# A hybrid decoder step on one core: the input's load order and the cost figures of the host scheduler

## The chip, the core and the metric

The kernel runs on one core of a Trainium2 chip. The metric is the device time of one execution in microseconds (us). Three runs of the kernel before gave 2321.42 to 2325.67 us, with a median of 2323.08 us.

## What is computed

One inference step of a decoder of two layers in float32, for one new sequence of 512 tokens (the prompt) and for eight running sequences with four new tokens each (the sample, 32 rows), which share all weights. Layer A runs sparse attention (compressed, selected and window branches) beside gated linear attention; layer C is a gated recurrence. Cut to what matters here:

```python
def layer_a(x, ...):
    h = rmsnorm(x, norm_w)
    q, kv, g_br, z_a, q_b, k_b, v_b, lr_b, z_b = split_cols(h @ w_in, A_SIZES)
    ...
    full = jnp.concatenate([past_kv, new_rows], axis=1)      # sample: 512 cached rows, in pages
    o_a = nsa_attend(q, gates, full, win_kv, ...) * jax.nn.silu(z_a)
    ...
    y = x + jnp.concatenate([o_a, o_b], axis=-1) @ w_out
def layer_c(x, ...):
    q, f, i, z = split_cols(rmsnorm(x, norm_w) @ w_in, C_SIZES)
    ...
    return x + o @ w_out, s
```

The model width is 2048, a cached page holds 128 rows, and `past_kv` is gathered through a page table whose entries are known only when the kernel runs.

## The kernel before

All 544 rows (512 prompt, 32 sample) go through each weight together. Activations lie transposed, in 16 k-tiles of 128 channels by 544 rows. Each operand of a product is split into a rounded part and a remainder (`xh`, `xl` for the activations, `wh`, `wl` for the weights), and each k-tile takes three products, in two column halves of 272: six TensorE (PE) instructions, named gm below. Weights come in tiles `wr` of 512 KB through SyncE's (SP) DMA queue, with three buffers; ScalarE (ACT) casts `wh`, VectorE (DVE) subtracts `wl`.

**The order.** A host-side list scheduler, the class `Kern`, emits the program. It keeps a modelled time for PE (`clk`), for the other engines (`et`) and for the tiles (`rdy`, `last`). `account` charges each instruction a modelled cost; a transfer gets an issue cost and a time on one shared `et["dma"]`. Side tasks (input, attention, recurrences) are generators that emit their next instruction when the model says that its operands are there, and the long runs of gm are emitted in between. So the figures of the model set the order of the instructions on each engine and nothing else: on the chip each engine works through its list in that order and waits on semaphores.

**The input.** `load_x` loads one quarter (512 channels) of the input as five tiles `xt`: four of the prompt (256 KB each) and one of the sample. `load0` and `load1`, at the first weight tiles of the first two blocks, call it. `input_task` transposes the quarters on PE, copies them out (`res`), scales them by the norm weight (`xh`, `xl`), and squares them on ACT for the norm; the norm's factor is spread over partitions by products `dg,ones`. Before the first transposes PE runs 24 products of a tile of ones (`onesr`). Small parameters (`cvr`) come over GpSimd's (POOL) queue.

**The decode attention.** `decode` attends from the sample to the cache at the end of layer A's projections, beside the last blocks of gm. It works through four items: two groups of sequences with paged rows (tile `pg`), then the same two with window rows (tile `pw`). An item transposes eight K tiles (`s<-ident,pg`), multiplies by the queries (`kct,qd`), takes the softmax, transposes the weights (`pd`) and multiplies eight V tiles in two halves (`pg,ptd`). At most `PAGES` = 9 tiles are in flight. `cache_tile` loads a `pg` tile as two DMAs of 128 KB on SP, each behind a read of its page number from the page table (`value_load`); the two paged items take 64 such DMAs. After it comes the output projection of layer A, whose operands (`oh`, `ol`) `parts_a` writes.

All engine calls pass through one helper, so their lines read L84; products are L211, transposes L215. The program after the change has 20 lines more above `input_task`'s callers, and there the two read L214 and L218.

Of the kernel before, what the change touches and what calls it, by code (L numbers as in the profile page):

```python
# [16 lines left out]
AF = mybir.ActivationFunctionType  # L17
# [3 lines left out]
P = 128  # L21
D = 2048
KT = D // P
TP = 512
# [39 lines left out]


LAT = 200.0
SQGAP = 900.0
COST = {"V": (62.0, 1.05), "A": (100.0, 0.84), "G": (110.0, 2.2), "S": (50.0, 0.0)}
FAST = {"tensor_scalar", "tensor_scalar_max", "memset"}

# [24 lines left out]
class Kern:  # L95
    def __init__(self, ctx, tc, a, o):
        self.ctx, self.tc = ctx, tc
        self.nc = Chip(self, tc.nc)
        self.a, self.o = a, o
        self.clk = 0.0  # L100
        self.et = {"V": 0.0, "A": 0.0, "G": 0.0, "S": 0.0, "dma": 0.0}
        self.rdy, self.last = {}, {}
        self.ring, self.held = {"s": [], "gm": []}, {}
        self.lanes, self.order = {}, []
        self.flags = set()
        self.uid = 0
        self.R = None
# [36 lines left out]
    def account(self, eng, op, args, kw):  # L144
        aps = [x for x in list(args) + list(kw.values()) if hasattr(x, "tensor") and hasattr(x, "shape")]
        if not aps or op in ("value_load", "preload_act_table_set"):
            return
        outs = [x for x in (kw.get("out", args[0] if args else None), kw.get("accum_out")) if x is not None]
        names = {x.name for x in outs}
        start = max([self.et[eng]] + [self.rdy.get(x.name, 0.0) + LAT for x in aps if x.name not in names]  # L150
                    + [max(self.rdy.get(x, 0.0), self.last.get(x, 0.0)) + LAT for x in names])
        n = 1
        for x in aps:
            k = 1
            for d in x.shape[1:]:
                k *= d
            n = max(n, k)
        if op == "dma_start":
            self.et[eng] = start + (1040.0 if eng == "G" else 60.0)
            self.et["dma"] = max(self.et["dma"], start) + n * outs[0].shape[0] * 4 / 300.0  # L160
            end = self.et["dma"] + 1900.0
        else:
            fix, per = COST[eng]
            if eng == "V" and op in FAST:
                per = 0.55
            if op == "reciprocal":
                per = 6.8
            end = self.et[eng] = start + fix + per * n
        for x in aps:
            self.last[x.name] = max(self.last.get(x.name, 0.0), end)  # L170
            if x.name in self.held and x.name not in names:
                self.held[x.name] -= 1
                if not self.held[x.name]:
                    del self.held[x.name]
        for x in names:
            self.rdy[x] = end

    def pe(self, cost, out, ins):
        start = max([self.clk] + [self.rdy.get(x.name, 0.0) + LAT for x in ins])
# [427 lines left out]
    def load_x(self, c):  # L607

        nc, a = self.nc, self.a
        for i in range(5):  # L610
            t = (self.r if c < 3 else self.g)("xt", [P, 512])
            s = slice(c * 512, (c + 1) * 512)
            if i < 4:
                nc.sync.dma_start(t, a["x_prompt"][0, i * P:(i + 1) * P, s])
            else:
                nc.sync.dma_start(t[:TS], a["x_sample"].rearrange("b t d -> (b t) d")[:, s])
            self.xt[(c, i)] = t

    def input_task(self):
# [6 lines left out]
        def squares(c, xt):  # L626
            junk = self.g("junk", [P, 512])
            for i in range(5):
                n = P if i < 4 else TS
                nc.scalar.activation(junk[:n], xt[i][:n], AF.Square, accum_out=ss[:n, i, c:c + 1])  # L630
                yield self.later(SQGAP)
            self.sqn += 1

        for c in range(4):
            xt = [self.xt.pop((c, i)) for i in range(5)]
            yield self.at(*xt)
            psb = self.bank(reads=4)
            for q in range(4):
                self.tr(psb[:, q * TS:(q + 1) * TS], xt[4][:TS, q * P:(q + 1) * P], self.ident[:TS, :TS])
            for q in range(4):  # L640
                kt = 4 * c + q
                yield self.at(banks=1)
                psa = self.bank()
                for i in range(4):
                    self.tr(psa[:, i * P:(i + 1) * P], xt[i][:, q * P:(q + 1) * P], self.ident)
                w = self.w_a[:, kt:kt + 1]
                hi, lo = self.g("xh", dt=F32R), self.g("xl", dt=F32R)
                res = self.g("res")
                self.cp(res[:, :TP], psa)
                self.cp(res[:, TP:T], psb[:, q * TS:(q + 1) * TS])  # L650
                self.scale(hi, res, w)
                nc.vector.scalar_tensor_tensor(lo, res, w, hi.bitcast(F32), op0=ALU.mult, op1=ALU.subtract)
                self.xhl[kt] = (hi, lo)
                self.store(self.xres[kt], res)
# [1105 lines left out]
    def layer_a(self):  # L1760
# [163 lines left out]
        def load0(i, t):  # L1924
            self.load_x(0 if i == 0 else 2)
            x0(i, t)
            if i == 0:
                self.small_loads()

        def load1(i, t):  # L1930
            x1(i, t)
            self.load_x(1 if i == 0 else 3)
        blocks[0].load, blocks[1].load = load0, load1
        blocks[0].now = True
        return blocks
# [85 lines left out]
    def program(self):  # L2021
# [25 lines left out]
        def parts_a():  # L2047
            gens = []
            for n, kt in enumerate(order_a):
                fl = [] if n < 4 else ["xfree"]  # L2050
                if kt >= 8:
                    gens.append(self.parts(kt, self.spill[kt], self.g, *fl))
                else:
                    gens.append(self.parts(kt, None, lambda s, dt=F32: self.r(s, dt=dt), "rmid"))
# [111 lines left out]
```

## Time and profile before

| what | us |
|---|---|
| median of three runs | 2323.08 |
| the profiled execution, its own time | 2324.13 |
| span of that execution's trace | 2322.4 |
| PE busy | 2288.0 |
| ACT busy | 1012.1 |
| DVE busy | 1394.5 |

The profiled execution is 1.05 us above the median and 1.7 us above its own span. The trace is read by engine: the timeline gives each stretch of like instructions with its start, its length and, in brackets, the idle time before it and what ended it. PE's instructions overlap, so the time of one is read from the starts of its neighbours.

### The profile page before, as it was taken

Reading aid. Unit: us, or ns where it says so; the run is one execution under the profiler, and the core shown is the slowest. Engines: PE = TensorE matmul, PEld = TensorE weight load, DVE = VectorE, ACT = ScalarE, POOL = GpSimd, SP = SyncE. Lnnn points to the kernel's source line nnn. Section 1 sums busy time; section 2 is a strip of 40 time slices with the busy share of each in tenths; the row PEclk is TensorE's granted clock in tenths of the full one; section 3 lists DMA queues with packets and bytes.
Section 4 is the critical chain, followed back from the end, with each engine's and each line's share of the span. In section 5 each row is a group of like instructions: output and inputs, shape, how many; then the busy total and the mean of one; then the engine's idle time right before and its main releaser. Section 6 shows DMA issues by size and latency. Waiting matters only on the chain.

```text
span 2322.4 us, 50208 instructions
## 1 busy us (share of the span) xinstructions
PE 2288.0 (99%) x20744; PEld 2231.0 (96%) x20744; DVE 1394.5 (60%) x2998; ACT 1012.1 (44%) x2105; POOL 33.5 (1%) x92
## 2 busy tenths in 40 slices
PE   8999999999999999999999999999999999999997
PEld 8999999999999999889999999999999999999997
DVE  5454577774664663454435777777777777775333
ACT  6343344443443443443333455444455444455333
POOL 4000000000000000000000000000000000000000
PEclk9999999999999999999999999999999999999999
DMA  7654434434113135754464333333333333333333
GB/s 238 165 158 143 125 95 110 116 102 131 46 51 88 47 108 158 217 156 134 138 197 142 102 88 108 93 93 101 97 98 93 93 94 102 93 98 120 107 101 115
DMA packets 429685, 270.69 MB, mean 117 GB/s; under 512 B 12326, under 2 KB 415632, under 8 KB 429328
## 3 DMA queue, kind: packets, MB, share of 16 engines
q1 hardware_dynamic: 428144, 256.65, 38.3%
q0 software_dynamic: 704, 8.72, 1.1%
q8 instruction: 163, 2.67, 0.5%
q10 hardware_dynamic: 608, 2.11, 0.2%
q14 instruction: 66, 0.54, 0.1%
HBM read 234.34 MB, written 41.42 MB: 119 GB/s over the span
## 4 chain that ended last, share of the span: by engine, by line
PE 93%; DMA 2%; ACT 1%; POOL 1%; DVE 1%; issue 1%; SPq 1%; DVEq 0%; POOLq 0%; ACTq 0%
PE gm L211 79%; PE s L211 11%; PE s L215 4%; DMA wr<-in_c_w_in_dram 1%; DMA pg<-in_cache_kv_dram 1%; SPq L84 1%; ACT junk L84 0%; DVE ol L84 0%; POOL mkt L84 0%; ACT wh L84 0%; POOL cvr L84 0%; ACT oh L84 0%; ACT e L84 0%; ACT res L84 0%; POOL lmb L84 0%
## 5 line engine op out<-in xcount | busy, mean ns | idle before, releaser
L211 PE MATMUL gm<-xh,wh 128*128 128x272 f32 x3744 | 802.5, 296 | 6.8 <-ACT wh L84 6.8
L211 PE MATMUL gm<-xh,wl 128*128 128x272 f32 x3744 | 775.8, 289 | 0.0
L211 PE MATMUL gm<-xl,wh 128*128 128x272 f32 x3744 | 775.5, 288 | 0.2
L84 DVE TENSOR_TENSOR wl<-wr,wh 128x512 fp32r<-128x512 f32 x660 | 450.5, 686 | 461.1 <-ACT wh L84 460.3
L211 PEld LDWEIGHTS gm<-xh,wh 128*128 128x128 f32 x3744 | 588.9, 189 | 19.4 <-ACT wh L84 7.8
L84 ACT CAST wh<-wr 128x512 fp32r<-128x512 f32 x660 | 401.3, 616 | 468.3 <-PE gm L211 436.0
L211 PEld LDWEIGHTS gm<-xl,wh 128*128 128x128 f32 x3744 | 588.2, 188 | 0.6 <-DVE xl L84 0.6
L211 PEld LDWEIGHTS gm<-xh,wl 128*128 128x128 f32 x3744 | 587.1, 188 | 0.8 <-DVE wl L84 0.6
L211 PE MATMUL gm<-oh,wh 128*128 128x272 f32 (+2 forms) x1024 | 218.3, 292 | 4.1 <-ACT oh L84 3.6
L211 PE MATMUL gm<-ol,wh 128*128 128x272 f32 (+2 forms) x1024 | 214.9, 289 | 0.5 <-DVE ol L84 0.5
L211 PE MATMUL gm<-oh,wl 128*128 128x272 f32 (+2 forms) x1024 | 215.2, 289 | 0.0
L211 PEld LDWEIGHTS gm<-oh,wh 128*128 128x128 f32 x1024 | 162.1, 189 | 5.5 <-ACT oh L84 4.0
L211 PEld LDWEIGHTS gm<-ol,wh 128*128 128x128 f32 x1024 | 162.3, 189 | 0.9 <-DVE ol L84 0.9
L211 PEld LDWEIGHTS gm<-oh,wl 128*128 128x128 f32 x1024 | 161.9, 189 | 0.0
L211 PE MATMUL gm<-ch,wh 128*128 128x258 f32 (+1 forms) x256 | 76.1, 297 | 0.0
L211 PE MATMUL gm<-ch,wl 128*128 128x258 f32 (+1 forms) x256 | 76.0, 297 | 0.0
L211 PE MATMUL gm<-cl,wh 128*128 128x258 f32 (+1 forms) x256 | 76.0, 297 | 0.0
L84 ACT ACTIVATE lv<-lv 128x512 f32<-128x512 f32 (+1 forms) x100 | 61.5, 634 | 29.6 <-DVE lv L84 28.5
L84 ACT COPY o<-s 128x32 f32<-128x32 f32 (+1 forms) x48 | 18.6, 387 | 127.7 <-PE s L211 127.7
L84 ACT ACTIVATE e<-e 128x544 f32<-128x544 f32 x96 | 63.1, 657 | 16.1 <-DVE e L84 14.0
L84 DVE TENSOR_TENSOR lv<-b 128x256 f32<-128x256 f32 (+2 forms) x160 | 68.9, 488 | 0.7
L84 DVE TENSOR_TENSOR rt<-gm,rt 128x544 f32<-128x544 f32 (+2 forms) x33 | 23.3, 707 | 63.7 <-PE gm L211 61.8
(382 smaller groups left out, 2552.4 us busy)
## 6 DMA issues: line engine op xcount, KB each, us to landing
wr<-in_c_w_in_dram SPq DMA_DIRECT2D x128, 512.0 KB
wr<-in_a_w_in_dram SPq DMA_DIRECT2D x104, 512.0 KB
pg<-in_cache_kv_dram SPq DMA_DIRECT2D x128, 128.0 KB
wr<-in_a_cmp_w_dram SPq DMA_DIRECT2D x32, 512.0 KB
wr<-in_a_w_out_dram SPq DMA_DIRECT2D x32, 512.0 KB
wr<-in_c_w_out_dram SPq DMA_DIRECT2D x32, 512.0 KB
out_dram<-s SPq DMA_DIRECT2D x48, 256.0 KB
pw<-in_cache_win_dram SPq DMA_DIRECT2D x32, 256.0 KB
```

The costliest lines, as they stand in the source:

```text
L84: return f(*args, **kw)
L211: return self.nc.tensor.matmul(out, lhsT, rhs, start=start, stop=stop, **kw)
L215: return self.nc.tensor.transpose(out, in_, ident, **kw)
```

## The change

The model: a DMA issue on SP or ACT costs 440 ns instead of 60; a DMA into a tile that is already being loaded no longer waits in the model for the one before it; POOL's DMAs no longer occupy the shared transfer time. The input: each quarter's sample tile is loaded first, two of the first quarter's prompt tiles are issued by ACT, and the last quarter is loaded right behind the third; squares are emitted only where the model's ACT is less than 300 ns ahead of PE; the first k-tile is scaled by ACT straight out of PSUM and 12 more `onesr` products follow its transposes. `parts_a` lets three parts instead of four go without waiting for `xfree`.

```diff
-SQGAP = 900.0
+SQGAP = 300.0
...
-        self.rdy, self.last = {}, {}
+        self.rdy, self.last, self.loading = {}, {}, set()
...
         start = max([self.et[eng]] + [self.rdy.get(x.name, 0.0) + LAT for x in aps if x.name not in names]
-                    + [max(self.rdy.get(x, 0.0), self.last.get(x, 0.0)) + LAT for x in names])
+                    + [max(self.rdy.get(x, 0.0), self.last.get(x, 0.0)) + LAT for x in names if x not in self.loading])
...
         if op == "dma_start":
-            self.et[eng] = start + (1040.0 if eng == "G" else 60.0)
-            self.et["dma"] = max(self.et["dma"], start) + n * outs[0].shape[0] * 4 / 300.0
-            end = self.et["dma"] + 1900.0
+            self.et[eng] = start + (1040.0 if eng == "G" else 440.0)
+            t = max(self.et["dma"], start) + n * outs[0].shape[0] * 4 / 300.0
+            if eng != "G":
+                self.et["dma"] = t
+            end = t + 1900.0
...
             self.rdy[x] = end
+            (self.loading.add if op == "dma_start" else self.loading.discard)(x)
...
-        for i in range(5):
+        for i in (4, 0, 1, 2, 3):
...
-                nc.sync.dma_start(t, a["x_prompt"][0, i * P:(i + 1) * P, s])
+                q = nc.scalar if c == 0 and i > 1 else nc.sync
+                q.dma_start(t, a["x_prompt"][0, i * P:(i + 1) * P, s])
...
                 n = P if i < 4 else TS
+                while self.et["A"] > self.clk + SQGAP:
+                    yield self.later(300.0)
                 nc.scalar.activation(junk[:n], xt[i][:n], AF.Square, accum_out=ss[:n, i, c:c + 1])
-                yield self.later(SQGAP)
+                yield self.later(300.0)
...
-            psb = self.bank(reads=4)
+            psb = self.bank(reads=4 if c else 5)
+            warm = self.bank() if c == 0 else None
...
-                psa = self.bank()
+                psa = self.bank(reads=2 if kt == 0 else 1)
...
-                self.cp(res[:, :TP], psa)
-                self.cp(res[:, TP:T], psb[:, q * TS:(q + 1) * TS])
-                self.scale(hi, res, w)
+                if kt == 0:
+
+                    nc.scalar.activation(hi[:, :TP], psa, AF.Copy, scale=w)
+                    nc.scalar.activation(hi[:, TP:T], psb[:, :TS], AF.Copy, scale=w)
+                    nc.vector.tensor_copy(res[:, :TP], psa)
+                    nc.vector.tensor_copy(res[:, TP:T], psb[:, :TS])
+                    for k in range(12):
+                        self.mm(warm[:, :P], self.onesr, self.onesr)
+                    nc.vector.tensor_copy(self.sm("warm", [P, 1], bufs=1), warm[:, 0:1])
+                else:
+                    self.cp(res[:, :TP], psa)
+                    self.cp(res[:, TP:T], psb[:, q * TS:(q + 1) * TS])
+                    self.scale(hi, res, w)
...
             if i == 0:
                 self.small_loads()
+            else:
+                self.load_x(3)
...
-            self.load_x(1 if i == 0 else 3)
+            if i == 0:
+                self.load_x(1)
...
-                fl = [] if n < 4 else ["xfree"]
+                fl = [] if n < 3 else ["xfree"]
```

**PE in the decode attention, between the two halves of the first item's V tiles.** Before, the first half (its last four products) is followed by gm:

```order
L211 MATMUL s_12105<-pg_11420,ptd_12048 32x256
L211 MATMUL s_12105<-pg_11766,ptd_12048 32x256
L211 MATMUL s_12105<-pg_11787,ptd_12048 32x256
L211 MATMUL s_12105<-pg_11821,ptd_12048 32x256
L211 MATMUL gm_12011<-xh_513,wh_12007 128x272 x2
L211 MATMUL gm_12011<-xl_514,wh_12007 128x272 x2
L211 MATMUL gm_12011<-xh_513,wl_12008 128x272 x2
```

and now by the second half's products:

```order
L214 MATMUL s_12045<-pg_11436,ptd_12035 32x256
L214 MATMUL s_12045<-pg_11752,ptd_12035 32x256
L214 MATMUL s_12045<-pg_11773,ptd_12035 32x256
L214 MATMUL s_12045<-pg_11807,ptd_12035 32x256
L214 MATMUL s_12045<-pg_11828,ptd_12035 32x256
L214 MATMUL s_12045<-pg_11863,ptd_12035 32x256
L214 MATMUL s_12045<-pg_11884,ptd_12035 32x256
L214 MATMUL s_12045<-pg_11923,ptd_12035 32x256
```

The 108 gm that stood between the halves have gone behind them. Over the whole stretch, from the first `s<-ident,pg` of `decode` to its last `pg,ptd`, PE's list holds 606 gm before and 234 now; the other 372 come later, and the count of page transposes and products is the same. The order of the 64 page DMAs on SP is the same too.

**DVE at the first k-tile.** Before:

```order
L84 COPY warm_248<-s_223 128x1
L84 COPY res_312<-s_300 128x32
L84 SCALAR_TENSOR_TENSOR xl_311<-res_312,wa,xh_310 128x544
L84 TENSOR_TENSOR wl_318<-wr_250,wh_317 128x512
L84 TENSOR_TENSOR wl_322<-wr_274,wh_321 128x512
```

and now:

```order
L84 COPY warm_248<-s_223 128x1
L84 COPY res_323<-s_316 128x512
L84 COPY res_323<-s_310 128x32
L84 COPY warm_340<-s_311 128x1
L84 SCALAR_TENSOR_TENSOR xl_322<-res_323,wa,xh_321 128x544
L84 TENSOR_TENSOR wl_344<-wr_250,wh_343 128x512
```

The 512-wide copy of `res` has come over from ACT, and the copy out of the bank of the 12 added products (`warm_340`) stands ahead of `xl`.

**SP at the start, around the third quarter's last tile.** Before, the fourth weight tile's neighbours are the stores of `res`; now the last quarter's loads stand between:

```order
L84 DMA wr_286<-in_a_w_in_dram 128x8x128
L84 DMA xt_298<-in_x_sample_dram 32x512
L84 DMA xt_300<-in_x_prompt_dram 128x512
L84 DMA xt_302<-in_x_prompt_dram 128x512
L84 DMA xt_304<-in_x_prompt_dram 128x512
L84 DMA xt_306<-in_x_prompt_dram 128x512
L84 DMA xres_74<-res_323 128x544
```

The five loads `xt_298` to `xt_306` have moved ahead of the stores of `res`, directly behind the third weight tile.

## Rows read from the trace of the kernel before

**Rows 1.** Page, parts 1 and 4: busy time by engine, and the chain that ended last.

```profile
PE 2288.0 (99%) x20744; PEld 2231.0 (96%) x20744; DVE 1394.5 (60%) x2998; ACT 1012.1 (44%) x2105; POOL 33.5 (1%) x92
...
PE 93%; DMA 2%; ACT 1%; POOL 1%; DVE 1%; issue 1%; SPq 1%; DVEq 0%; POOLq 0%; ACTq 0%
```

**Rows 2.** Waits of PE: engine, line, waited for: us in total, times, longest.

```profile
PE gm L211 <- ACT wh L84: 6.8, 4, 3.5
PE s L215 <- DMA pg<-in_cache_kv_dram: 5.0, 7, 1.5
```

**Rows 3.** Timeline of SP, page stage: start, us, engine, line, operation, tile, count.

```profile
867.71 13.24 SPq L84 DMA_DIRECT2D pg<-in_cache_kv_dram  x12
881.05 0.37 SPq L84 DMA_DIRECT2D spill<-y  x1
...
937.44 6.36 SPq L84 DMA_DIRECT2D pg<-in_cache_kv_dram  x6
```

**Rows 4.** Instructions of SP by kind, 867 to 881 us: duration ns min/median/max.

```profile
L84 SPq TENSOR_LOAD <-ptab x12: 263/268/443, 866.7 to 879.9; - x12
...
L84 SPq DMA_DIRECT2D pg<-in_cache_kv_dram x12: 332/333/356, 867.7 to 880.6; - x12
```

**Rows 5.** Timeline of PE over the same stage.

```profile
861.46 0.60 PE L215 MATMUL s<-ident,pg 128*128 128x128 f32 x4
...
878.34 0.41 PE L211 MATMUL gm<-xh,wl 128*128 128x272 f32 x2
878.59 0.41 PE L211 MATMUL gm<-xh,wh 128*128 128x272 f32 x2
...
886.77 1.07 PE L211 MATMUL s<-pg,ptd 128*32 128x256 f32 x16
...
954.54 1.07 PE L211 MATMUL s<-pg,ptd 128*32 128x256 f32 x16
```

**Rows 6.** Timeline of SP, earlier page loads.

```profile
176.87 8.20 SPq L84 DMA_DIRECT2D pg<-in_cache_kv_dram  x8
```

**Rows 7.** Timeline of PE, first matmul held up by those loads.

```profile
187.76 0.33 PE L215 MATMUL s<-ident,pg 128*128 128x128 f32 x1 [1.46 <-DMA pg<-in_cache_kv_dram]
```

**Rows 8.** Timeline of PE at the start; in brackets the idle time before and its releaser.

```profile
3.32 5.38 PE L211 MATMUL s<-onesr 128*128 128x128 f32 x24
...
12.94 0.66 PE L211 MATMUL gm<-xl,wh 128*128 128x272 f32 x2
...
14.03 2.76 PE L215 MATMUL s<-ident,xt 128*128 128x128 f32 x12
...
27.76 0.52 PE L211 MATMUL gm<-xh,wh 128*128 128x272 f32 x2 [0.98 <-ACT wh L84]
...
32.62 0.52 PE L211 MATMUL gm<-xh,wh 128*128 128x272 f32 x2 [0.41 <-ACT wh L84]
...
36.83 1.43 PE L215 MATMUL s<-ident,xt 32*128 32x32 f32 x12 [1.07 <-ACT junk L84]
```

**Rows 9.** Timeline of ACT at the start.

```profile
26.47 0.63 ACT L84 ACTIVATE junk<-xt 128x512 f32<-128x512 f32 x1 [2.57 <-POOL ss L84]
...
50.32 0.61 ACT L84 ACTIVATE junk<-xt 32x512 f32<-32x512 f32 x1
```

**Rows 10.** Timeline of SP, page loads after the start.

```profile
80.19 8.81 SPq L84 DMA_DIRECT2D pg<-in_cache_kv_dram  x8
```

**Rows 11.** Timeline of PE, start of the output projection of layer A.

```profile
1015.01 0.51 PE L211 MATMUL gm<-oh,wh 128*128 128x272 f32 x2 [1.94 <-ACT oh L84]
1015.77 0.52 PE L211 MATMUL gm<-ol,wh 128*128 128x272 f32 x2 [0.24 <-DVE ol L84]
...
1017.34 0.66 PE L211 MATMUL gm<-oh,wh 128*128 128x272 f32 x2
```

**Rows 12.** Timeline of PE, start of layer C.

```profile
1232.51 0.82 PE L211 MATMUL gm<-xh,wh 128*128 128x272 f32 x2 [3.46 <-ACT wh L84]
...
1234.04 0.66 PE L211 MATMUL gm<-xh,wh 128*128 128x272 f32 x2
```

## Prediction

> **What bounds the kernel.** I read the page first, then PE's waits, then the timelines of the stretches that the change reorders. PE is busy for 2288.0 us of the span and makes 93% of the chain that ended last [rows 1], so the time is PE's fixed work plus its idle time plus what a low clock costs. The change adds 12 small products to PE's work and removes none; it can only move idle time. The largest waits of PE are 6.8 us for `wh` and 5.0 us for pages [rows 2]. Those page waits lie early (one is shown below); in the decode attention, from 861 to 956 us, PE waits for no page. There gm, which need only weights, stand between the steps that need pages. Elsewhere the instructions keep their order, so I cost two stretches: the start, up to about 90 us, and the decode attention with what follows it.
>
> **Decode attention: PE's side.** From its first page transposes at 861.46 to the end of its last page products at 955.5 PE takes 94.1 us [rows 5]. A pair of gm starts 0.25 us after the pair before it (878.34, 878.59), so one is 125.5 ns. The new order leaves 372 fewer gm in this stretch: 372 x 0.1255 = 46.7 us. If nothing made it wait, PE would pass through the stretch in 94.1 - 46.7 = 47.4 us, and would reach its last page products at 46.4 us, counted from the first transposes. The 372 gm are still done, later; by themselves they cost nothing.
>
> **Decode attention: SP's side.** After the first 18 page DMAs, 46 more are issued, from 867.71 on, in the same order as before [rows 3]. A page DMA is 0.33 us of issue, a read of the page number (0.27) and register instructions [rows 4]; 12 take 13.24 us, so the spacing is (13.24 - 0.33)/11 = 1.17 us, and in the last six (6.36 - 0.33)/5 = 1.21 [rows 3]. The eight at 176.87 give (8.20 - 0.33)/7 = 1.12 [rows 6]. I take 1.16. About five other issues stand between (weights and spills, some 0.44 us each, 0.37 in the row at 881.05 [rows 3]): 2.2 us. The last page DMA is then issued at 867.71 + 45 x 1.16 + 2.2 + 0.3 = 922.4. For its landing: the eighth of the DMAs from 176.87 was out by 185.07 and PE went on behind the last page it waited for at 187.76 [rows 6, 7], so at most 2.7 us; I take 2.5. The page is there at 924.9, or 63.4 us into the stretch, and PE wants it at 46.4. PE waits 63.4 - 46.4 = **17 us**, spread over the second halves of both items' V tiles and the second item's K tiles. Time lost at an earlier page is not lost again at a later one, so the last page alone counts.
> Bounds: SP issues the 19th DMA when a tile comes free, which the earlier transposes may make sooner by up to 6.2 us (867.71 against 861.46); that gives +10. At 1.24 us a page, above the slowest row, it is 45 x 0.08 = 3.6 more: +20.
>
> Before, the scheduler's model made the second DMA into a tile wait for the first and so spread the steps far apart; the new model takes 440 + 400 = 840 ns for a page and 46 x (1.16 - 0.84) = 15 us too little, which is the same amount.
>
> **The window items behind it.** Their DMAs need no page number; PE's steps stand closer there too. Two or three short waits, +0.5 (0 to 2).
>
> **Output projection.** Before, the attention's end overlaps it: a wait of 1.94 for `oh` after the last attention transposes, 0.24 for `ol`, then pairs of gm at 0.45 instead of 0.25 us apart for about 3.5 us, which costs 1.7 [rows 11]. Now the attention ends before it. The stall may go entirely (-2.2 - 1.7 = -3.9), or the parts, which now queue together on DVE and ACT, stall as much (+1). I take -1, since DVE has to make all of them just there.
>
> **The start.** Three waits go if the reorder works: 0.98 and 0.41 for `wh`, 1.07 for the last quarter behind the squares (36.83) [rows 8]. The first square waits 2.57 us on POOL and holds up ACT's casts [rows 9]; now it is issued later, when POOL is done, and ACT casts first. With the products that ran late around these waits it is up to 3.6; I take -3 (0 to -3.6).
> The 12 added products run at the first level of the clock: 24 took 5.38 us [rows 8], so 12 take 2.7, from about 10.2, when the first k-tile's transposes end, to 12.9; the first product stood at 12.32. `xl` stands behind the copy out of their bank: 12.9 + 0.3 + 0.8, so the product that needs it starts at 14.0 against 12.94 [rows 8]: **+1.1** (0 if ACT's shorter path lets them overlap).
> The squares are spread out, so the last is later than 50.32 [rows 9], and the norm's products, which had no wait, get one: +1 (0 to 2). On SP the stores of new rows come behind groups of page loads that take 8.81 us for eight [rows 10], and DVE waits for their buffers: +1 (0 to 2.1).
> Two queues for the first quarter gain nothing: until 8.7 PE is in the 24 `onesr` products [rows 8], and the tiles are there by then. Together the start gives about **0**, from -4 to +3.
>
> **The clock.** PE's clock starts at the lower level, 1.2 GHz: 12 transposes from 14.03 take 2.76 us [rows 8], where four at the upper one, 2.4 GHz, take 0.60 [rows 5], three fours 1.8 at most. After the wait of 3.46 us at the start of layer C pairs of gm are 0.45 apart instead of 0.25 until about 1238.6, some 3.4 us lost [rows 12]; after 1.94 it was 1.7 [rows 11]. The waits for pages will reach some 3 us in one piece, so the clock falls there too. While PE waits for SP anyway a slow gm costs little; behind the last wait it does: **+1.5** (0 to 5).
> The Trainium skill's page "TensorE: Matmul & The Clock Gate", Part 1, says that the throttled level is the default and that activity releases it. The rows after both waits agree with it; by it the 12 added products at the start should bring the rise earlier, though the 24 before them ran wholly at the low level here. What that would give, worked out from rows: the 12 transposes from 14.03 in 1.8 instead of 2.76, -1, which the start's lower end holds.
>
> **The sum.** 17 + 0.5 - 1 + 0 + 1.5 = +18 against the profiled execution's 2324.1, which makes 2342.1. That execution stands 1.05 above the median of the runs, 2323.08; in terms of the median I predict **2341 us**. A measurement of this kernel tells 0.2%, 4.6 us, from no change.
>
> **Rivals.**
> 1. *The pages keep up (faster).* The last page is needed 46.4 us in; with 45 DMAs, 2.2 of other issues, 6.25 of lead and 2.8 to issue and land, that holds from a spacing of (46.4 - 11.2)/45 = 0.78 us down. Then the decode waits and their clock loss vanish, and the start and the projection decide: 2323.1 - 3.5 for the start, where its costs come out low, and -1 to -3.9 for the projection: 2316 to 2319. Against it: every group of page DMAs stands at 1.12 to 1.21 [rows 3, 6], and at that spacing PE did wait early in the program [rows 2, 7]. 0.10.
> 2. *The clock stays low through the page waits.* PE does about 47 us of work there in pieces between waits. If gm stay 0.2 us a pair too slow beyond what SP's pace hides, and again at the output projection, 4 to 8 us more come: about 2347. For it: both longer waits of before brought the clock down [rows 11, 12]. Against: the waits of 0.98 and 1.07 at the start did not stretch the products behind them for long. 0.16.
> 3. *SP runs ahead and the projection's stall goes.* The 19th DMA goes out several us sooner, and -3.9 is had at the projection: 18 - 5, and another 2.9 off for -3.9 in place of -1: +10, about 2333. SP's list holds weights before the 19th DMA, which wait for buffers that PE frees in its own time; that speaks against. 0.12.
> 4. *The change does not do what it says.* The loads that are meant to come sooner bring nothing where PE is busy anyway, as in the first 8.7 us [rows 8], and the page waits of the new order are hidden after all; then the terms of the start cancel: 2320 to 2326. PE's stretch before is full of work without a wait, and what stood between the pages is gone, so I see no cover. 0.05.
> My forecast has 0.57. Rival 1 lies mostly below 2318.4 and rival 4 mostly between that and 2327.7: faster 0.10, same 0.05, slower 0.85. The range takes in the forecast with its bounds (+10 to +20 for the pages; the other terms partly against each other) and rivals 2 and 3: 2329 to 2350.
>
> **What would show it.** In the changed profile PE should wait for `pg` some 15 us in 10 to 14 pieces, between about 875 and 925, each piece about the spacing of SP's page DMAs (0.6 to 1.1) with a few of 2 to 3; SP's page DMAs should stand at the same 1.12 to 1.21 with hardly a gap; the next 390 gm and the output projection should follow without attention steps. At the start the waits at 27.76 and 36.83 should be gone and the first `xl` product near 14. I am wrong if PE has no page waits there, if SP's spacing falls below 0.8, or if SP stands idle between page DMAs waiting for buffers, which would make the wait longer than SP's issue alone.

## The result and the profile after

The changed kernel takes 2345.95 us (median; 2344.56 to 2350.95, 4 runs) against 2323.44 for the kernel before in the same sessions: ratio 1.0102, with a 95% interval of 1.009 to 1.0115. The forecast was 2341 and slower; the range, 2329 to 2350, holds the result.

The profiled execution is the longest of the four, 2350.95, 5.0 above the median; the others show a granted clock of 0.992 to 0.993 where it shows 0.991. So its sums go against its own time: 2350.95 - 2324.13 = 26.8 us to be found, where the medians are 22.5 apart; some 4 are particular to the two profiled executions.

The page of the changed kernel, first its busy times, then the chain:

```profile
PE 2301.8 (98%) x20756; PEld 2240.6 (95%) x20756; DVE 1396.9 (59%) x2999; ACT 1012.7 (43%) x2106; POOL 33.3 (1%) x92
...
PE 92%; DMA 3%; SPq 2%; DVE 1%; issue 1%; ACT 1%; DVEq 0%; ACTq 0%
```

PE is busy 13.8 us more [rows 1], where the 12 products take 2.8: the rest is for the most part work done at the lower clock. PE's waits:

```profile
PE s L218 <- DMA pg<-in_cache_kv_dram: 13.8, 15, 2.6
PE s L214 <- DMA pg<-in_cache_kv_dram: 6.2, 5, 1.8
PE gm L214 <- ACT wh L84: 4.4, 1, 4.4
PE gm L214 <- ACT oh L84: 3.2, 2, 1.6
...
PE gm L214 <- DVE ol L84: 1.5, 2, 1.3
```

Waits for pages went from 5.0 us to 13.8 + 6.2 = 20.0 [rows 2]; the new ones stand on transposes (L218) and on the V products (L214). SP in the decode attention, its timeline:

```profile
871.33 0.37 SPq L84 DMA_DIRECT2D wr<-in_a_w_in_dram  x1
872.54 18.04 SPq L84 DMA_DIRECT2D pg<-in_cache_kv_dram  x16
890.68 0.37 SPq L84 DMA_DIRECT2D spill<-y  x1
891.15 0.39 SPq L84 DMA_DIRECT2D wr<-in_a_w_in_dram  x1
892.78 17.94 SPq L84 DMA_DIRECT2D pg<-in_cache_kv_dram  x16
...
912.69 8.62 SPq L84 DMA_DIRECT2D pg<-in_cache_kv_dram  x8
...
923.34 6.43 SPq L84 DMA_DIRECT2D pg<-in_cache_kv_dram  x6
```

The pages stand at (18.04 - 0.33)/15 = 1.18 us, as before [rows 3], and from 872.54 on they run on with only weight and spill issues between: SP is the engine that hardly rests. PE over the same stretch, its timeline with the idle time and its releaser in brackets:

```profile
865.17 0.60 PE L218 MATMUL s<-ident,pg 128*128 128x128 f32 x4
...
886.79 0.62 PE L214 MATMUL s<-pg,ptd 128*32 128x256 f32 x2 [1.56 <-DMA pg<-in_cache_kv_dram]
889.16 0.64 PE L214 MATMUL s<-pg,ptd 128*32 128x256 f32 x8 [1.75 <-DMA pg<-in_cache_kv_dram]
...
896.57 0.82 PE L218 MATMUL s<-ident,pg 128*128 128x128 f32 x2 [2.61 <-DMA pg<-in_cache_kv_dram]
...
906.11 0.33 PE L218 MATMUL s<-ident,pg 128*128 128x128 f32 x1 [1.51 <-DMA pg<-in_cache_kv_dram]
...
930.27 0.64 PE L214 MATMUL s<-pg,ptd 128*32 128x256 f32 x8 [1.68 <-DMA pg<-in_cache_kv_dram]
931.75 1.06 PE L214 MATMUL s<-pg,ptd 128*32 128x256 f32 x2 [0.84 <-DMA pg<-in_cache_kv_dram]
932.74 1.08 PE L214 MATMUL s<-snk,ptn 32*32 32x256 f32 x8
```

PE stands still for pages ten times in the stretch, 12.2 us, and is through with the last page at 932.74. And the granted clock, by stretches (us, PE busy, ..., PEclk, DMA share, GB/s):

```profile
66.00:76.00 10.00, 8.22 (x54) 7.80 (x53) 3.62 (x6) 3.32 (x7) 0.00 (x0) 0.83 0.23 70
186.00:198.00 12.00, 10.29 (x70) 9.86 (x69) 7.56 (x13) 6.40 (x11) 0.00 (x0) 0.86 0.34 108
...
861.00:880.00 19.00, 19.00 (x156) 17.02 (x155) 10.50 (x21) 6.90 (x13) 0.00 (x0) 1.00 0.64 184
880.00:894.00 14.00, 10.23 (x79) 6.71 (x78) 2.63 (x9) 1.91 (x6) 0.00 (x0) 0.88 0.43 131
894.00:921.00 27.00, 21.11 (x139) 17.65 (x140) 7.12 (x14) 6.87 (x12) 0.00 (x0) 0.81 0.49 150
...
928.00:1003.00 75.00, 72.49 (x601) 62.96 (x598) 31.37 (x74) 27.23 (x51) 0.00 (x0) 0.95 0.62 181
```

Between 880 and 921, and again behind 928, the clock is at its lower level, 1.2 GHz, for a part. The DMA engines are half idle (0.43, 0.49) while PE waits for DMAs. (The first two rows are early stretches, behind waits for the first pages; the first experiment comes back to them.)

The sum for this execution, from the starts of the same instruction in both traces: the first page transposes of `decode` stand at 865.17 against 861.46, **+3.7** for all that is ahead. From there to the end of the V products (932.74) it is 67.6 us, where the work alone is 47.4: **+20.2**, of which 12.2 are waits and the other 8 mostly PE's work drawn out at the lower clock while SP's pace holds it anyway. The first product of the output projection stands at 1033.32 against 1003.49, and before 3.3 us of attention steps were still to come there, so 26.5: **+2.6** for the window items and the low clock around 935. Then the waits of the output projection:

```profile
1041.09 0.52 PE L214 MATMUL gm<-oh,wh 128*128 128x272 f32 x2 [1.56 <-ACT oh L84]
1042.88 0.52 PE L214 MATMUL gm<-ol,wh 128*128 128x272 f32 x2 [1.27 <-DVE ol L84]
```

The first of them stood at 1015.01 in the kernel before [rows 11], so 26.1, and behind its `ol` and the low clock of before it is 25.4: **-1.1** for the projection. **+1.4** come behind 2142, in a stretch that the change does not touch: PE waits there 1.63 us, in the kernel before 1.62, and only in the changed trace does the clock fall behind it. Together 26.8.

### The profile page after: what moved, and what is told of

It reads as the page before. It is cut to its first block, busy times and chain, and to the rows that moved or that the text cites. A ratio compares the mean times of both kernels' runs of the same rounds, so it can differ in the third digit from the quotient of the medians.

```text
span 2349.3 us, 50242 instructions
## 1 busy us (share of the span) xinstructions
PE 2301.8 (98%) x20756; PEld 2240.6 (95%) x20756; DVE 1396.9 (59%) x2999; ACT 1012.7 (43%) x2106; POOL 33.3 (1%) x92
## 4 chain that ended last, share of the span: by engine, by line
PE 92%; DMA 3%; SPq 2%; DVE 1%; issue 1%; ACT 1%; DVEq 0%; ACTq 0%
PE gm L214 78%; PE s L214 11%; PE s L218 4%; SPq L84 2%; DMA wr<-in_c_w_in_dram 1%; DMA pg<-in_cache_kv_dram 1%; DVE ol L84 1%; DMA wr<-in_a_w_in_dram 0%; DMA xt<-in_x_sample_dram 0%; DMA rt<-xres 0%; DVE wl L84 0%; ACT e L84 0%; ACT oh L84 0%; DMA out_dram<-snt 0%; DVE e L84 0%
## 5 line engine op out<-in xcount | busy, mean ns | idle before, releaser
L214 PE MATMUL gm<-xh,wh 128*128 128x272 f32 x3744 | 805.9, 297 | 4.6 <-ACT wh L84 4.4
L214 PE MATMUL gm<-xl,wh 128*128 128x272 f32 x3744 | 778.9, 290 | 0.7 <-DVE xl L84 0.7
L214 PE MATMUL gm<-xh,wl 128*128 128x272 f32 x3744 | 778.6, 289 | 0.4 <-issue 0.4
L214 PEld LDWEIGHTS gm<-xh,wh 128*128 128x128 f32 x3744 | 591.4, 190 | 17.8 <-issue 8.9
L214 PEld LDWEIGHTS gm<-xl,wh 128*128 128x128 f32 x3744 | 590.3, 189 | 1.3 <-DVE xl L84 1.2
L214 PEld LDWEIGHTS gm<-xh,wl 128*128 128x128 f32 x3744 | 590.5, 189 | 0.6 <-DVE wl L84 0.5
L214 PE MATMUL gm<-oh,wh 128*128 128x272 f32 (+2 forms) x1024 | 217.9, 292 | 3.7 <-ACT oh L84 3.2
L214 PE MATMUL gm<-ol,wh 128*128 128x272 f32 (+2 forms) x1024 | 215.5, 289 | 1.5 <-DVE ol L84 1.5
L214 PE MATMUL gm<-oh,wl 128*128 128x272 f32 (+2 forms) x1024 | 215.0, 289 | 0.0
L214 PEld LDWEIGHTS gm<-oh,wh 128*128 128x128 f32 x1024 | 161.8, 189 | 4.6 <-ACT oh L84 3.6
L214 PEld LDWEIGHTS gm<-ol,wh 128*128 128x128 f32 x1024 | 162.3, 189 | 1.9 <-DVE ol L84 1.9
L214 PEld LDWEIGHTS gm<-oh,wl 128*128 128x128 f32 x1024 | 162.3, 189 | 0.0
L214 PE MATMUL gm<-ch,wh 128*128 128x258 f32 (+1 forms) x256 | 76.1, 297 | 0.0
L214 PE MATMUL gm<-ch,wl 128*128 128x258 f32 (+1 forms) x256 | 76.1, 297 | 0.0
L214 PE MATMUL gm<-cl,wh 128*128 128x258 f32 (+1 forms) x256 | 76.0, 297 | 0.0
```

The lines of the kernel that those rows point to most:

```text
L214: return self.nc.tensor.matmul(out, lhsT, rhs, start=start, stop=stop, **kw)
```

## Experiments

Medians below are compared with the kernel before on the same chip, 2323 to 2324 us in each session. The diffs are against the changed kernel unless said otherwise.

**1. The input alone.** `account` as it was before the change, all else changed:

```diff
-            self.et[eng] = start + (1040.0 if eng == "G" else 440.0)
-            t = max(self.et["dma"], start) + n * outs[0].shape[0] * 4 / 300.0
-            if eng != "G":
-                self.et["dma"] = t
-            end = t + 1900.0
+            self.et[eng] = start + (1040.0 if eng == "G" else 60.0)
+            self.et["dma"] = max(self.et["dma"], start) + n * outs[0].shape[0] * 4 / 300.0
+            end = self.et["dma"] + 1900.0
```

(and the two lines on `loading` gone). 

> The changed input code with the old model of transfers. PE's order in the decode attention is that of before (606 gm from the first page transposes to the last page products). Theory (the 20 us of the decode stage come from the new order against SP's pace of 1.17 us a page DMA): no page wait there; the start alone decides: about -3 for the waits that went between 24 and 38 us, +1.1 for the 12 products, 0 to +1 for the norm's products: 2319 to 2323 us. Rival A (the changed start sets the rest of the program off, for instance by the clock): the +3.4 us that stand at 235 us in the changed trace stay, about 2327. Rival B (the input's load order disturbs the page loads): page waits in the decode stage and about 2346.

Measured: 2320.74 us, ratio 0.9993 (0.9983 to 1.0003), so no difference that this measurement can tell, with a median 2.8 below. Its windows of the decode stretch show PE without a gap at the full clock:

```profile
60.00:100.00 40.00, 40.00 (x329) 39.58 (x328) 17.74 (x37) 15.52 (x30) 2.28 (x3) 1.00 0.51 148
861.00:956.00 95.00, 95.00 (x795) 87.27 (x795) 40.19 (x81) 38.10 (x70) 0.00 (x0) 1.00 0.62 181
```

The theory holds: the slowdown is not in the input's code. In its trace the decode stage starts at 857.75, 3.7 us earlier than before, in the changed kernel 3.7 us later: the new model costs 7.4 us ahead of that stage. The first pages, in 60 to 100 us, have no wait here; in the changed kernel there are waits of 0.38 and 1.40 and the low clock behind them:

```profile
70.54 0.33 PE L218 MATMUL s<-ident,pg 128*128 128x128 f32 x1 [1.40 <-DMA pg<-in_cache_kv_dram]
```

The reason is again the order: between the first page transpose of the program and the 32nd PE's list holds 42 gm in the changed kernel, 156 here and 150 before. By the work that PE has done at the same time in both traces (an estimate), some 4.5 of the 7.4 us are lost by 100 us, and the rest behind the page waits from 130 to 200 us.

**2. One rule undone.** Only this line goes back:

```diff
-                    + [max(...) + LAT for x in names if x not in self.loading])
+                    + [max(...) + LAT for x in names])
```

> The change without the one rule that a DMA into a tile being loaded no longer waits in the model for the one before it. PE's list then has 612 gm between the first page transposes and the last page products of decode, as before (606). Theory (that rule alone drew the steps together): PE's stretch is 18 us + 612 x 0.1255 = 94.8 us again, SP's 67 us are hidden: no page wait in the stage, and 2346 less 20 to 24 = 2322 to 2326 us. Rival A (the 440 ns of issue or the POOL rule did it): 2340 to 2346. Rival B (DMA bandwidth, not order): unchanged.

Measured: 2339.93 us, 1.0079 (1.0062 to 1.0095). A miss. The waits inside the page stage are nearly gone, as expected (2.2 us are left), but two others came: page waits of 5.1 us from 70 to 83 us, and one at the output projection. PE's timeline there:

```profile
1015.41 0.41 PE L214 MATMUL gm<-oh,wl 128*128 128x272 f32 x2
1020.27 1.33 PE L218 MATMUL s<-ident,pd 128*128 128x128 f32 x5 [4.45 <-ACT pd L84]
...
1021.85 0.66 PE L214 MATMUL gm<-ol,wh 128*128 128x272 f32 x2
```

PE waits 4.45 us for the last softmax (`pd`): the window items have been spread past the last gm of the input projection, and nothing stands ready to fill in. Behind it PE runs at 0.45 us a pair. So an estimate that brings pages too late costs time as well; the tenth experiment gives the amount, 7.5 us.

**3. The price of a page raised.**

```diff
-            self.et["S"] += 400.0
+            self.et["S"] += 1000.0
```

> The change with a modelled page DMA of 440 + 1000 ns instead of 440 + 400, all else kept. PE's list has 450 gm between the first page transposes and the last page products. Theory: PE's own work in the stretch is 18 + 450 x 0.1255 = 74.5 us, SP needs 67: page waits of 0 to 2 us there, no long stretch at the low clock, 2346 less 18 to 22 = 2324 to 2328 us. Rival A (the size of the shift does not matter, the attention's early end stalls the output projection): page waits shrink but the projection takes them over, 2335 to 2342. Rival B (bandwidth): page waits stay over 8 us, 2340 and more.

Measured: 2330.28 us, 1.0035 (1.0023 to 1.0048); 15.7 of 22.5 us are back. No page wait is left in the stage, as the theory had it, one of 1.22 for a window tile is. The stage costs 0.5 us above its work. The rest, which the expectation missed by 2 us and more: waits of 1.87 for a page at 70 and of 1.85 behind the row stores at 88, so that the stage starts at 863.49, 2.0 later than before and 5.7 later than in the first experiment. At the projection stand 1.67 and 1.16 with the low clock behind them, where 1.94 and 0.24 with a low clock stood before [rows 11].

**4. A second queue, same order.** PE's list is that of the change.

```diff
+            q = eng if k == 0 or slot < 2 else self.nc.gpsimd
-            page = eng.value_load(self.ptab[0:1, i:i + 1], min_val=0, max_val=39)
+            page = q.value_load(self.ptab[0:1, i:i + 1], min_val=0, max_val=39)
```

(with `q.dma_start`, charged to SP in the model so that nothing moves). 

> The change with PE's order kept (234 gm in the stretch), but every second page DMA of decode, with its read of the page number, issued by POOL instead of SP. Theory (SP's issue pace is the limit): SP issues 23 instead of 46 DMAs, 27 us instead of 54, before PE wants the last page at 46: page waits in the stage under 1 us, and the low-clock stretch of 13.7 us from 880 to 894 goes: 2346 less 20 to 24 = 2322 to 2326 us. Rival A (the transfers themselves, bandwidth or landing, are the limit): page waits stay over 10 us and the time stays over 2340. Rival B (POOL is no faster a way: its issue takes over 2 us a page): half the wait stays, about 2335.

Measured: 2330.84 us, 1.0032 (1.0019 to 1.0044). SP and the one wait that is left in the stage:

```profile
871.62 8.79 SPq L84 DMA_DIRECT2D pg<-in_cache_kv_dram  x8
...
882.61 8.98 SPq L84 DMA_DIRECT2D pg<-in_cache_kv_dram  x8
```

```profile
888.17 0.44 PE L221 MATMUL s<-ident,pg 128*128 128x128 f32 x2 [1.67 <-DMA pg<-in_cache_kv_dram]
```

SP still takes (8.79 - 0.33)/7 = 1.21 us a page, but issues half of them, and of 12.2 us of page waits 1.67 is left. That settles SP against the transfers themselves. The time missed its expectation by 5 us: the waits at 71, 88 and the projection (2.10, 0.87) are like those of the third experiment, and the stage starts at 864.25.

**5. The best version: input as changed, old model, early pages over two queues.** Against the first experiment:

```diff
+            q = self.nc.gpsimd if k == 1 and slot < 2 else eng
...
```

(with the read of the page number and the DMA on `q`, charged to SP in the model as in the fourth).

> The changed input code with the old model of transfers (the first experiment, 2320.74 us), and every second page DMA of the compressed branch, before the decode attention, issued by POOL with its read of the page number. Theory (SP's pace of 1.17 us a page holds up PE there too): the six page waits between 126 and 244 us, 4.6 us in all, shrink to under 1: 2316.5 to 2318 us, 5 to 7 below the kernel before. Rival A (these waits are for landing, not for issue): no change, 2320.7. Rival B (POOL's issue is slower than SP's or comes behind its small loads): the waits move or grow, 2321 to 2326.

Measured: 2312.94 us (2310.7 to 2314.55), 0.9957 (0.9943 to 0.997): faster than both kernels, and by more than expected. PE's waits:

```profile
PE gm L214 <- ACT oh L84: 3.6, 2, 1.9
...
PE gm L214 <- ACT wh L84: 1.4, 1, 1.4
```

There is no row for `pg` any more, where 5.0 us stood before [rows 2]. At the decode stage this trace is 9.6 us ahead of the kernel before, 5.9 more than the first experiment's. At the end it is 13.3: layer C's start waits 1.41 instead of 3.46 us [rows 12] and keeps the clock. The twelfth shows that this is not owed to the kernel's order.

**6. Constant page numbers.** PE's list is that of the change, and decode's pages are fetched by constants, so that this kernel reads other rows than the page table asks for, of the same size:

```diff
-            page = eng.value_load(self.ptab[0:1, i:i + 1], min_val=0, max_val=39)
+            page = None if slot > 1 else eng.value_load(...)
...
-            eng.dma_start(t[:, k, :], rows[bass.ds(page, 1), :, slot, :].rearrange("o p c -> (o p) c"))
+            src = rows[bass.ds(page, 1), :, slot, :] if page is not None else rows[i:i + 1, :, slot, :]
+            eng.dma_start(t[:, k, :], src.rearrange("o p c -> (o p) c"))
```

> The change with PE's order kept, in which decode loads pages by constant numbers instead of those of the page table, so its page rows are others than asked for; the read of the page number goes, and SP alone issues all. Theory (issue pace, made of the read and the register instructions around it): SP's spacing falls from 1.17 to about 0.44 us, the last page lands before PE wants it, page waits in the decode stage under 1 us: 2346 less 18 to 22 = 2324 to 2328 us, at most a few us below the run with two issuing queues (2330.84). Rival A (bandwidth: 128 KB every 0.44 us beside the weights is too much): the spacing falls but landings take longer, page waits of 3 us and more, 2332 and up. Rival B (what the second queue saved was not issue time): 2340 and up.

Measured: 2326.52 us, 1.0014 (1.0004 to 1.0023). SP alone:

```profile
869.50 8.81 SPq L84 DMA_DIRECT2D pg<-in_cache_kv_dram  x16
...
879.35 9.30 SPq L84 DMA_DIRECT2D pg<-in_cache_kv_dram  x16
```

The spacing is (8.81 - 0.33)/15 = 0.57 us, somewhat over the expected 0.44, and no page wait stands in the stage. So 0.6 of the 1.17 us a page are the read of the number and what goes with it, and the same transfers can come at twice the pace.

**7. Issue cost back at 60 ns.**

```diff
-            self.et[eng] = start + (1040.0 if eng == "G" else 440.0)
+            self.et[eng] = start + (1040.0 if eng == "G" else 60.0)
```

> The change with the modelled issue cost of a DMA back at 60 ns. PE's list has 198 gm between the first page transposes and the last page products, 36 fewer than in the change. Theory (each gm that leaves the stretch uncovers its 125.5 ns of SP's pace): 36 x 0.1255 = 4.5 us more of page waits: 2350 us, 2348 to 2352. Rival A (the wait is already as large as SP's queue allows and the rest goes elsewhere): same as the change, 2346. Rival B (the 440 ns is what slowed the program): 2324 to 2335.

Measured: 2354.97 us, 1.0138 (1.0123 to 1.0154): 9.0 over the change where 4.5 were expected, in the right direction. The traces do not show where all of the 9.0 come from: the two profiled executions, 2353.83 and 2350.95, are only 2.9 apart. Between them the stage costs 22.4 us above its work instead of 20.2, with more of it at the low clock:

```profile
880.00:905.00 25.00, 17.36 (x102) 11.16 (x100) 4.14 (x11) 2.70 (x7) 0.00 (x0) 0.68 0.46 140
```

0.68 over 25 us is most of the stretch at 1.2 GHz. The first window tile is then waited for 2.11 us. At 88 us PE waits 3.60 behind the row stores instead of 0.27, but the waits at 69 and 71 are gone, and the stage starts at 865.37, as in the change. Why the medians are 9.0 apart stays open.

For the stage itself these runs give a dose. Its length less its work (47.4 us with 234 gm, 125.5 ns more or less for each gm) is 22.4 us with 198 gm, 20.2 with 234, 0.5 with 450, and nothing with 606, in the first experiment and the tenth. For the whole program the count alone does not decide: the second and the tenth, with 612 and 606 gm, take 2339.93 and 2332.47, for what they lose among the first pages and at the projection.

**8 and 9. Without the added products.** The eighth takes the 12 products out of the first experiment's kernel; the scheduler then moves other instructions. The ninth leaves one of the 12 in the fifth's kernel, and the model charges 12:

```diff
                     for k in range(12):
-                        self.mm(warm[:, :P], self.onesr, self.onesr)
+                        if k == 0:
+                            self.mm(warm[:, :P], self.onesr, self.onesr)
+                        else:
+                            self.pe(109.0, warm[:, :P], (self.onesr, self.onesr))
```

> The first experiment (2320.74 us) without the 12 added products and the copy behind them. Theory (they delay the first weight products by 1.1 us and bring the clock's rise no earlier): -0.5 to -1.2, 2319.5 to 2320.2 us, and the granted clock rises at the same time as with them. Rival A (they bring the rise earlier, and without them the following products run longer at the lower level): 2321 to 2323 us. Rival B (the product behind waits for its weights anyway): no difference.

Measured: 2324.55 us, 1.0007 (0.9996 to 1.0019), 3.8 over the first.

> The fifth experiment (2312.94 us) with one of the 12 added products left, the model still charging 12, so that no other instruction moves (in the run without them the reads of the small parameters had moved forward and were waited for, 3.8 us). Theory (the products delay the first weight products by 1.1 us and do nothing else): the product with xl starts near 12.7 instead of 13.8, 2311.5 to 2312.2 us, unless the following quarters' loads take the gain back. Rival A (they bring the clock's rise forward): the rise comes later than at 18 and the time is 2313 to 2315. Rival B (gain taken back by the next wait): 2312.9, with a new wait of about 1 us between 15 and 40.

Measured: 2318.69 us, 0.9978 (0.9969 to 0.9988), 5.8 over the fifth (in the two traces 5.5 stand at the start of the decode stage, 857.29 against 851.84). Both theories were wrong on the whole. PE's timeline of the ninth:

```profile
12.83 0.82 PE L214 MATMUL gm<-xl,wh 128*128 128x272 f32 x2
...
27.83 0.26 PE L218 MATMUL s<-ident,cvr 75*128 75x75 f32 x1 [0.79 <-ACT res L84]
...
31.59 0.24 PE L218 MATMUL s<-ident,per 64*128 64x64 f32 x1 [2.27 <-DMA per<-in_a_cmp_pe_dram]
...
32.67 0.66 PE L214 MATMUL gm<-xh,wh 128*128 128x272 f32 x2
```

The product with `xl` does come a microsecond earlier (12.83 against 13.79 with all 12). But then PE waits 2.27 us for `per`, a small load on POOL, and the clock falls. The loads, by the DMA view of 14 to 36 us (KB each, us to landing), in the ninth and then in the fifth:

```profile
per<-in_a_cmp_pe_dram POOLq DMA_DIRECT2D x1, 32.0 KB, 4.5
```

```profile
per<-in_a_cmp_pe_dram POOLq DMA_DIRECT2D x1, 32.0 KB, 1.9
```

What differs ahead of it is the order against the next weight load. The ninth's timelines of SP and POOL, then the fifth's:

```profile
26.57 0.38 SPq L84 DMA_DIRECT2D wr<-in_a_w_in_dram  x1
26.99 0.56 POOL L84 DMA_DIRECT2D per<-in_a_cmp_pe_dram  x1 [1.15 <-DMA cvr<-in_c_norm_dram]
```

```profile
26.56 0.56 POOL L84 DMA_DIRECT2D per<-in_a_cmp_pe_dram  x1 [0.16 <-issue]
27.19 0.38 SPq L84 DMA_DIRECT2D wr<-in_a_w_in_dram  x1
```

All fourteen traces go by this: the last of POOL's small loads lands in 1.7 to 2.1 us where it is issued ahead of that weight load (the kernel before, the first, fifth and twelfth experiments) and in 4.3 to 5.1 where it is issued behind it (the other ten, the changed kernel with all 12 products among them).

**10. Only the POOL rule left of the new model** (the second experiment with 60 ns). 

> The second experiment (no rule for tiles being loaded, 2339.93 us) with the modelled issue cost of a DMA back at 60 ns; of the change to the model only the POOL rule is left. PE's list has 606 gm in the decode stretch, as before. Theory (there the 440 ns on top of the old rule made pages look too late, so that the attention's end came after the last gm of layer A and PE waited 4.45 us for pd): that wait goes, the stage from 853 to 1018 us costs what it did before, and 2340 less 11 to 12 = 2328 to 2329 us, the rest being page waits between 70 and 83 us. Rival A (those early waits too come from the 440 ns): 2321 to 2323. Rival B (the POOL rule causes all of it): 2338 to 2340.

Measured: 2332.47 us, 1.0035 (1.0023 to 1.0048). The wait for `pd` is gone and the stage costs what it did before; the total is some 4 us above the expectation, with page waits of 5.9 us between 70 and 84. So the 440 ns caused the second experiment's loss at the projection, and taking POOL's DMAs out of the modelled transfer time is enough to bring the first pages too close.

**11 and 12. The late load moved.** `per` is issued as the first of POOL's small loads, in the ninth's and the fifth's kernel; no other instruction moves:

```diff
         q = nc.gpsimd
+        pes = self.g("per", [P, P])[:64]
+        q.dma_start(pes, a["a_cmp_pe"].rearrange("o s l d -> (o s l) d"))
...
-        pes = self.g("per", [P, P])[:64]
-        q.dma_start(pes, a["a_cmp_pe"].rearrange("o s l d -> (o s l) d"))
```

> The ninth experiment (2318.69 us; one of the 12 products) with one DMA moved on POOL: the position rows (per, 32 KB) are loaded as the first of the small parameters instead of the last; all other instructions stand where they did. In the ninth per took 4.5 us to land, beside weights and the last quarter, against 1.9 to 2.0 with the 12 products, and PE waited 2.27 us for it, then ran 3.4 us at the low clock. Theory (PE came a microsecond earlier to a load that came later because of the traffic it had set off): per lands before 26, its wait goes, and the 1.1 us at the first products are kept: 2318.7 less 2.3 to 5.5 = 2313 to 2316 us. Rival A (the 12 products help through the clock, not through the loads): no change, 2318 to 2319. Rival B (another small load is waited for in its place, cvr): a wait of 1 to 2 us at the transposes of cvr, 2316 to 2318.

Measured: 2316.07 us (2312.37 to 2319.11), 0.9968 (0.9955 to 0.998).

```profile
27.88 0.26 PE L218 MATMUL s<-ident,cvr 75*128 75x75 f32 x1 [1.14 <-DMA cvr<-in_a_cmp_b_dram]
...
29.30 0.27 PE L218 MATMUL s<-ident,per 64*128 64x64 f32 x1
```

The wait for `per` is gone, 2.6 us came back, and 1.14 for `cvr`, the next small load, took a part: theory and second rival together. In the trace the decode stage starts at 852.60, so at that point 4.7 of the 5.5 us are back. What these two traces differ by beyond that lies behind it, where the clock falls in one and not in the other.

> The fifth experiment (2312.94 us; all 12 products) with the same move of per on POOL. Theory (there per had landed in time, so its place matters nothing): 2312 to 2314 us. Rival (the other small loads come 0.5 us later and cvr is waited for): 2314 to 2315.

Measured: 2313.38 us (2313.1 to 2317.29), 0.9957 (0.9944 to 0.997): no difference from the fifth, as expected. Its profiled execution (2317.29) waits 3.36 us at layer C's start and the clock falls there, with PE's instructions in the fifth's order: what the fifth's trace gained at that place differs between executions.

## Why the prediction was right

- **What bounds the kernel, and the direction.** PE's fixed work plus idle time; the longest stretch that changed is decode's, and PE there waits for SP's page issue. Experiments 4 and 6 show it from both sides: with PE's order kept, a second issuing queue or a cheaper issue takes the stage's page waits from 12.2 us to 1.7 and to none. Rival 1's price, 0.78 us a page, agrees with it: at 0.57 the waits vanish.
- **Decode attention, +17.** Measured +20.2 in the profiled execution, 12.2 of it as waits where some 15 were forecast, because the low clock draws out the work between them. The spacing was right (1.16 taken, 1.18 measured). Mis-sized were the start of the 19th DMA, 7.4 us into the stage instead of 6.25 (872.54 - 865.17), and the "other issues": each pause of SP costs more than its row, as from 890.58 to 892.78 for two issues. The lower bound's idea, an earlier 19th DMA, did not come about: SP's list holds weights ahead of it (871.33), as the third rival's "against" said.
- **The clock, +1.5, and the window items, +0.5.** Together 2.6 measured behind the last page, and part of the 20.2. The clock fell where the text said. That it costs a varying amount fits the runs, whose granted clock of 0.991 goes with the longest time and 0.992 to 0.993 with the others, but was not shown by stage.
- **Output projection, -1.** Measured -1.1, but by luck: the waits did not shrink (1.56 + 1.27 instead of 1.94 + 0.24); only the low clock behind them stayed away. In the seventh experiment, with 1.58 + 1.25, it did not.
- **The start, 0.** This step failed: +3.7. The parts came near where they were read from rows: some -3.6 for the waits from 24 to 38 us, where -3 was taken, and +0.75 at the first products (13.69 against 12.94 [rows 8] for the product with `xl`), where +1.1 was. Missed was that the new model packs the *first* pages too, between 60 and 75 us (42 gm among them instead of 150); the text looked for the stores' wait on SP (0.27 us in the changed trace) and for the norm's products there (no wait), not for pages and the clock. The first experiment puts what the model costs ahead of the decode stage at 7.4 us.
- **The sum.** The misses add up instead of cancelling: +3.2 for the stage, +0.6 behind it, +3.7 for the start, and 1.4 behind 2142 that no term held. The median came out 5 us above the forecast; it was the width of the range that held it.
- The two queues for the first quarter were not tried by themselves; that they bring nothing is only argued from PE's being busy until 8.6.

## What to carry to other kernels

When a scheduler's cost model is changed, read its new price against the trace's spacing of that very operation (0.84 against 1.17 us here), and count what now stands between the steps that use it: the count, times the duration, is the cover that was given away. A model that was wrong in two ways may have been right in sum; mending one of them can give a worse order: with the POOL rule alone the tenth experiment takes 2332.47 us, where the old model takes 2320.74 with the same input. And where an engine issues a queue of small DMAs behind register reads, a second, idle engine's queue can be tried first: with every second early page on POOL the first experiment's kernel gained 7.8 us (2320.74 to 2312.94).

## What was not expected

Doing the first products a microsecond earlier made the program 5.8 us slower. That the 12 idle products bring the clock up sooner shows in no trace: by their record of the granted clock it rose between 16.9 and 19.8 us where all 12 ran, at 15.4, 16.5 and 18.9 in the three traces without them or with one, and at 16.7 in the kernel before. (The Trainium skill's page "TensorE: Matmul & The Clock Gate", Part 1, has activity release the throttle; that 12 more products would bring that forward, as the prediction weighed, no trace here shows.) What they do in the fifth experiment is hold PE back, and with it the next weight load, until POOL's last small load has been issued: `per` took 1.9 us to land with them and 4.5 without. In the changed kernel the weight load is ahead of `per` all the same, `per` takes 5.1 us, and PE, which wants it only at 39.69, does not wait. Moving that load gave 2.6 us back by the medians and 4.7 of 5.5 by the start of the decode stage, which shows the load's part; that the traffic of the weight load is what slows it is argued from the order and the landing times, with no experiment on it.
